# Three weight tiles of the first stage in buffers of another pool

## The chip, the cores and the metric

The kernel runs on one NeuronCore of a Trainium2 chip. A time is the device time of one execution in microseconds (us). The kernel before was timed three times: 1133.57, 1134.46 and 1135.39 us, median 1134.46. TensorE is called PE (its weight loads PEld), VectorE DVE, ScalarE ACT, GpSimd POOL. SyncE (SP) computes nothing here: it issues most of the DMAs, in the order of its own instruction stream, and what it waits for holds up every DMA behind it.

## The reference, cut to what matters

One layer of a backbone over 640 tokens (512 of a noisy grid, 128 of a prompt), width 1024, all in float32. What matters is the beginning:

```python
m = silu(cvec) @ w_ada + b_ada                  # modulation: 1024 -> 6 * 1024, for two vectors c and c_ctx
sh1, sc1, g1, sh2, sc2, g2 = split(m, 6)
h = rmsnorm(x, norm1_g) * (1.0 + sc1) + sh1
u_rw, u_na, gate_rw, gate_na = split(h @ p["w_in"], IN_SPLITS)
q, k, v = split(u_na, 3)                        # then the recurrence over u_rw, neighbourhood attention over q, k, v,
                                                # the merge, and a feed-forward block
```

The first stage needs only `sh1` and `sc1`, 2048 columns of `w_ada`: 8 MB of weights for two vectors. `h` is the input of every projection that follows.

## The kernel before, in words

Products of large matrices are done in three passes of a split float32: a weight tile of 512 KB is loaded into `wst` (`wdma`, L176), rounded by ACT into `whi` (L194), and what is left goes into `wlo` on DVE (L197); `h` is split likewise, into `hh` (ACT, L434) and `hl` (DVE, L436 and L438). There are two `wst` buffers.

**The first stage** (`with s0`). The modulation of `sh1` and `sc1` is cut by columns into three parts, `ada_part(k0, n, c0)`: part one covers the feature blocks 0 and 1 of the eight, part two blocks 2 and 3, part three blocks 4 to 7. Each part runs over all eight blocks of the inner dimension. Parts one and two load four tiles `wa` each (a tile holds two blocks of the inner dimension and comes in two DMAs of 256 KB), part three loads eight (one DMA of 512 KB each, `kt` 0 to 7). All have the tag `wa` of the stage's pool, with eight buffers (`WAB`): parts one and two take the eight, and tiles 0 to 3 of part three go where the tiles of part one were, tiles 4 to 7 where those of part two were. Each tile is used by one group of matmuls of PE into `psa` (`ada_mm`, L263). When a part is complete, `mod_part` copies its rows (L418), transposes them (L421), makes the coefficients A and B (L424, L427) and writes that part of `hh` and `hl`.

Between these groups PE does the first projection, q: `qg` is a generator of its matmuls (L313), four weight chunks of two inner blocks each, 60 matmuls for the first two chunks. `PRM["qp"]` says how many of them stand between two groups. In part two these are 0, 0, 7, 6 and 7, in part three 2, 5, 4, 4, 3, 2, 5, 3 and 1: the group of tile 0 follows the 2, that of tile 1 the 5, and so on, and the weights of the second q chunk are asked for between tiles 2 and 3. The third chunk needs blocks 4 and 5 of `h`, so it comes after part three.

**What sets the order.** In this stage PE's order is written by hand (`tc.manual_schedule(engines={PE})`). The order of SP, ACT, DVE and POOL is written by the framework's planner, ahead of the run: it goes through the program with times of its own, and gives an engine the instruction that comes first in the program among those that it holds to be ready. A DMA whose buffer is free can so stand far ahead of its place in the program. After the first stage comes the rest of q, k and v (planner's order on PE too), then attention, recurrence and feed-forward, where orders written by hand prevail; SP's is the planner's throughout.

**The recurrence's pool** `nf` is opened before the first stage. It has two buffers `f5` and one `nk5`, each of 128 x 1280 float32. Their first users before the change: `upw`, 256 KB of small weights (`prep_dma`, L617, in `nk5`; read by `prep_cast` in the eighth step of attention), and half of each of the first two weight tiles of the modulation's later columns (`ada_w`, L1027, in `f5`, 512 KB each; read by PE at L1046 from the first steps of attention on). The table `rpbp` comes in windows `win` of 124.5 KB (L860).

Of the kernel before, what the change touches and what calls it, by code (L numbers as in the profile page):

```python
# [7 lines left out]
F32 = mybir.dt.float32  # L8
# [6 lines left out]
P = 128  # L15
# [7 lines left out]
XB, WAB, FA, SF = 4, 8, 2, 16  # L23
# [87 lines left out]
def V(ap, dims, off=0):  # L111

    return bass.AP(ap.tensor, ap.offset + off, [list(ap.ap[0])] + [list(d) for d in dims])
# [3 lines left out]
def body(ctx: ExitStack, tc: tile.TileContext, xs, xp, cols, consts, w_ada, b_row, w_rw, w_qkv,  # L117
# [5 lines left out]
    def open_pool(stack, name, bufs=1, space=None):  # L123
        if space is None:
            return stack.enter_context(tc.tile_pool(name=name, bufs=bufs, reuse_waits="tile"))
        return stack.enter_context(tc.tile_pool(name=name, bufs=bufs, reuse_waits="tile", space=space))

    def right_pool(stack, name):
        return stack.enter_context(tc.tile_pool(name=name, bufs=1, reuse_waits="tile", side="right"))
# [14 lines left out]
    def nm(s):  # L144
        cn[0] += 1
        return f"{s}_{cn[0]}"
# [189 lines left out]
        dve.tensor_scalar(out=D[:, dqg:dqg + 1], in0=col("qg"), scalar1=0.125, scalar2=None,  # L336
                          op0=ALU.mult)


    hs = ExitStack()  # L340
    weights(ctx, WST, 2)
    o, mt = [], []
# [22 lines left out]
    nf = open_pool(nstack, "nf")  # L365
    nk_t = lambda n, shape: nf.tile(shape, F32, tag="nk5", bufs=1, name=nm(n))
    f5 = lambda: nf.tile([P, 1280], F32, tag="f5", bufs=2, name=nm("f5"))
    sb = open_pool(s1, "p1")
    p1 = sb
    kcT = sb.tile([P, 4, 128], F32, name="kcT")  # L370
# [5 lines left out]
    sb = right_pool(s0, "p0")  # L376
# [11 lines left out]

    def wa_load(k0, n, kt):

        w = sb.tile([P, 1024], F32, tag="wa", bufs=WAB, name=nm("wa"))
        for i in range(4 // n):
            wv = w_ada[(kt + i) * 128:(kt + i + 1) * 128, 0:2048].rearrange("p (g c) -> p g c", g=2)
            sp.dma_start(V(w[:, :], [[128 * n, 2], [1, 128 * n]], i * 256 * n), wv[:, :, 128 * k0:128 * (k0 + n)])
        return w

    def ada_part(k0, n, c0):

        for kt in range(0, 8, 4 // n):
            w = wa_load(k0, n, kt)  # L400
            yield
            for i in range(4 // n):
                ada_mm(psa, w[:, i * 256 * n:(i + 1) * 256 * n], kt + i, 64 * n, c0)
# [438 lines left out]
    with s1:  # L842

        s1.enter_context(s1l)
        sb = right_pool(s1l, "p1l")
# [90 lines left out]
        with ExitStack() as s1b:  # L936
# [128 lines left out]
            with tc.manual_schedule(engines=FIRST):  # L1065
                for k, step in enumerate(PRM["na"].split()):
                    a, p, b, q, n, s_ = (int(x) for x in (step + ".0").split(".")[:6])
# [31 lines left out]
    with ExitStack() as s3:  # L1099
        sb = open_pool(s3, "p3")  # L1100
# [653 lines left out]
    def add_gated(ps, i, n, c, a=0, b=512):  # L1754
# [15 lines left out]
                      name=f"b{x[0]}{x[1]}{i}") for i in range(2)] for x in halves2}  # L1770
    sb = open_pool(ctx, "p4")
# [466 lines left out]
    with tc.manual_schedule(engines=FIRST):  # L2238
# [8 lines left out]
        for part, fs in enumerate(fts):  # L2247
# [3 lines left out]
            for j, ft in enumerate(todo):  # L2251
# [13 lines left out]
                n = len(todo)  # L2265
# [114 lines left out]
def _build(arrays):  # L2380
    import concourse.bacc as _bacc

    nc = _bacc.Bacc("TRN2", target_bir_lowering=False, num_devices=1)
    args = [nc.dram_tensor(f"in_{n}_dram", v.shape, mybir.dt.from_np(v.dtype), kind="ExternalInput").ap()
            for n, v in arrays.items()]
    args += [nc.dram_tensor(f"out_{i}_dram", s, F32, kind="ExternalOutput").ap()
             for i, s in enumerate(_OUTS)]
    with tile.TileContext(nc, **TCARGS) as tc:
        body(tc, *args)
    return nc  # L2390
# [12 lines left out]
```

## Time and profile before

| | before |
|---|---|
| time, median of 3 runs | 1134.46 us |
| the profiled execution's own time | 1134.67 us |
| its span, first to last instruction | 1132.8 us |
| PE busy | 1099.7 us, 97% |
| DVE, ACT, POOL busy | 72%, 50%, 22% |
| mean granted clock of PE | 0.995 |
| bytes moved, mean rate | 179.05 MB, 158 GB/s |
| DMA in the stretch from 10 to 41 us | 16 engines busy throughout, 375 GB/s |

Busy time is the union of an engine's instructions; PE's ends are modelled, so its busy time is an upper bound of its work. A timeline gives the start in us from the first instruction, the duration, engine and line, the operation with what it writes and reads, how many are merged in the row, and in brackets how long the engine stood idle before and what ended that. "SPq" is the issue of a DMA, not its transfer.

### The profile page before, as it was taken

To read this page: it belongs to the slowest core of one execution; us is meant where nothing else is said; L and a number is where in the kernel's file an instruction comes from. 1 tells how busy PE (TensorE), PEld (TensorE's weight loads), DVE (VectorE), ACT (ScalarE), POOL (GpSimd) and SP (SyncE) were. 2 spreads that over 40 slices of the span, in tenths; PEclk is the share of its full clock that TensorE was granted. 3 is DMA by queue.
4 is the path that set the end of the run, shared out by engine and by line. 5 is a ranking of instruction groups with operands and counts; after the bars stand their busy time and mean duration, and the time that the engine had idled before them with its cause. 6 is when DMAs were issued, how large, how long until landed. Compare 5 with 4: busy or idle time off the path is not lost. (4 is left out here: it accounts for less than half of the span.)

```text
span 1132.8 us, 27124 instructions
## 1 busy us (share of the span) xinstructions
PE 1099.7 (97%) x11118; PEld 970.9 (86%) x11118; DVE 814.6 (72%) x1709; ACT 571.7 (50%) x1106; POOL 246.3 (22%) x318
## 2 busy tenths in 40 slices
PE   6999999999999999999999999999999999999998
PEld 4688878889888988888898788998999989989987
DVE  4565465668648947956697846899788888889854
ACT  4445566665566575467543524554453543444430
POOL 1163235321101111210100431152212122131200
PEclk8999999999999999999999999999999999999999
DMA  9753677645423353353643873377567567665622
GB/s 341 264 108 104 186 258 266 211 138 127 118 57 96 105 141 91 96 134 81 248 139 108 260 222 130 131 178 191 135 181 181 143 158 174 181 165 139 158 84 93
DMA packets 72995, 179.05 MB, mean 158 GB/s; under 512 B 8708, under 2 KB 23684, under 8 KB 72872
## 3 DMA queue, kind: packets, MB, share of 16 engines
q1 hardware_dynamic: 58488, 140.86, 37.8%
q0 software_dynamic: 12368, 33.56, 16.2%
q10 hardware_dynamic: 2016, 2.90, 0.8%
q8 instruction: 87, 1.43, 0.5%
q14 instruction: 36, 0.29, 0.1%
HBM read 137.81 MB, written 16.94 MB: 137 GB/s over the span
## 5 line engine op out<-in xcount | busy, mean ns | idle before, releaser
L1932 PE MATMUL f<-t,whi 128*128 128x320 f32 x640 | 141.8, 309 | 1.1 <-ACT whi L1977 0.8
L1932 PE MATMUL f<-b,whi 128*128 128x320 f32 x608 | 135.0, 310 | 0.4 <-DVE b L214 0.4
L225 PE MATMUL fl<-h,whi 128*128 128x320 f32 x672 | 122.5, 321 | 0.7 <-ACT U L542 0.7
L1932 PEld LDWEIGHTS f<-t,whi 128*128 128x128 f32 x640 | 106.8, 188 | 1.9 <-ACT whi L1977 1.3
L225 PEld LDWEIGHTS fl<-h,whi 128*128 128x128 f32 x672 | 101.2, 188 | 6.0 <-ACT U L542 0.9
L1932 PEld LDWEIGHTS f<-b,whi 128*128 128x128 f32 x608 | 101.8, 188 | 1.2 <-issue 0.6
L1932 PE MATMUL f<-t,wlo 128*128 128x320 f32 x320 | 99.0, 309 | 0.2 <-DVE wlo L1980 0.2
L1932 PE MATMUL f<-b,wlo 128*128 128x320 f32 x304 | 94.0, 309 | 0.1
L194 ACT CAST whi<-wst 128x1024 fp32r<-128x1024 f32 (+1 forms) x67 | 68.9, 1030 | 39.1 <-PE acc L313 27.1
L313 PE MATMUL acc<-whi,h 128*128 128x512 f32 x240 | 79.3, 404 | 0.3 <-DVE h L438 0.3
L1977 ACT CAST whi<-ws 128x1024 fp32r<-128x1024 f32 x40 | 42.1, 1052 | 68.7 <-PE f L1932 42.2
L197 DVE TENSOR_TENSOR wlo<-wst,whi 128x1024 fp32r<-128x1024 f32 (+2 forms) x47 | 48.1, 1033 | 26.0 <-ACT whi L194 25.8
L193 POOL DMA_DIRECT2D wlo<-wst x28 | 24.9, 889 | 183.7 <-ACT wlo L192 168.0
L225 PE MATMUL fl<-h,wlo 128*128 128x320 f32 x336 | 62.3, 317 | 0.0
L1932 PEld LDWEIGHTS f<-t,wlo 128*128 128x128 f32 x320 | 60.1, 188 | 0.5 <-DVE wlo L1980 0.5
L1991 POOL TENSOR_TENSOR ws<-wst 128x512 f32<-128x512 f32 x20 | 31.8, 1589 | 120.9 <-DVE wlo L1980 81.6
L1932 PEld LDWEIGHTS f<-b,wlo 128*128 128x128 f32 x304 | 57.1, 188 | 0.4 <-DVE wlo L1980 0.4
L1980 DVE TENSOR_TENSOR wlo<-ws,whi 128x1024 fp32r<-128x1024 f32 x40 | 53.7, 1343 | 4.1 <-ACT whi L1977 4.1
L313 PEld LDWEIGHTS acc<-whi,h 128*128 128x128 f32 x240 | 45.3, 191 | 12.7 <-issue 2.4
L1475 DVE TENSOR_TENSOR ZV<-w,Dt 64x128 f32<-64x128 f32 x64 | 18.5, 289 | 52.0 <-PE w L1463 50.9
L225 PEld LDWEIGHTS fl<-h,wlo 128*128 128x128 f32 x336 | 51.2, 188 | 1.8
L984 POOL TENSOR_TENSOR L<-L,m 128x384 f32<-128x384 f32 (+1 forms) x40 | 32.1, 824 | 93.8 <-DVE m L983 75.8
(379 smaller groups left out, 2826.4 us busy)
## 6 DMA issues: line engine op xcount, KB each, us to landing
wst<-in_w_dram SPq DMA_DIRECT2D x58, 512.0 KB
wst<-in_w_rw_dram SPq DMA_DIRECT2D x31, 512.0 KB
wlo<-wst POOLq DMA_DIRECT2D x28, 512.0 KB, 4.6
wa<-in_w_ada_dram SPq DMA_DIRECT2D x24, 512.0 KB
f<-in_w_ada_dram SPq DMA_DIRECT2D x16, 512.0 KB
t<-in_w_dram SPq DMA_DIRECT2D x16, 512.0 KB
wst<-in_w_qkv_dram SPq DMA_DIRECT2D x12, 512.0 KB
o<-o_d SPq DMA_DIRECT2D x14, 320.0 KB
```

The lines of the kernel that those rows point to most:

```text
L193: pool.dma_start(lo[:, :n].bitcast(F32), st[:, :n], accum_op=ALU.add)
L194: act.copy(hi[:, :n], st[:, :n])
L197: dve.tensor_tensor(out=lo[:, a:b], in0=st[:, a:b], in1=hi[:, a:b].bitcast(F32), op=ALU.subtract)
L225: pe.matmul(ps[:, :t1 - t0], w[:, a:a + 128], x[:, k0 + kt, t0:t1], start=n == 0, stop=n == 3 * nk - 1)
L313: pe.matmul(pss[i][:, a:b], lhs(x, kt, ts_), w[:, cs_], start=ki == 0 and n == 0, stop=ki == last and n == 2)
L984: pool.tensor_tensor(out=L, in0=L, in1=V(m[:, :], [[0, w]], 3), op=ALU.mult)
L1475: dve.tensor_tensor(out=V(ZV[own, l + 1, h, :], [[128 * dl, 2], [1, 64]]), in0=V(pn[own, :], [[64, 2], [1, 64]], 64 * g), in1=V(Dt[own, 0, ...
L1932: pe.matmul(ps[:, :H2], w_[:, c_], x_[:, kt, :], start=first and kt + n == 0, stop=last and kt == 3 and n == 2, skip_group_check=more)
L1977: act.copy(r[0][:, :width], src())
L1980: dve.tensor_tensor(out=r[1][:, :width], in0=src(), in1=r[0][:, :width].bitcast(F32), op=ALU.subtract)
L1991: eng_x(PRM["se"][i - 1]).tensor_tensor(out=o_, in0=x, in1=y, op=op)
```

## The change

The loader of the modulation's tiles, `wa_load`, takes the buffers of tiles 4, 5 and 6 of part three (`n == 4` is part three) from the pool `nf`: tiles 4 and 5 are the first users of the two buffers `f5`, tile 6 is the first of `nk5`. Of each the first 1024 columns are used. The other five tiles of part three stay in the stage's pool, where tile 7 now is the fifth and not the eighth that asks for a buffer again. `upw` and the two `f` tiles become the second users of their buffers, and wait for the groups of matmuls that read tiles 6, 4 and 5. Sizes of pools, transfers and the work of all engines are the same.

```diff
     nk_t = lambda n, shape: nf.tile(shape, F32, tag="nk5", bufs=1, name=nm(n))
     f5 = lambda: nf.tile([P, 1280], F32, tag="f5", bufs=2, name=nm("f5"))
+    late_home = (f5, f5, lambda: nk_t("wa", [P, 1280]))
...
     def wa_load(k0, n, kt):
 
-        w = sb.tile([P, 1024], F32, tag="wa", bufs=WAB, name=nm("wa"))
+        w = late_home[kt - 4]()[:, 0:1024] if n == 4 and 3 < kt < 7 else sb.tile([P, 1024], F32, tag="wa", bufs=WAB, name=nm("wa"))
         for i in range(4 // n):
             wv = w_ada[(kt + i) * 128:(kt + i + 1) * 128, 0:2048].rearrange("p (g c) -> p g c", g=2)
             sp.dma_start(V(w[:, :], [[128 * n, 2], [1, 128 * n]], i * 256 * n), wv[:, :, 128 * k0:128 * (k0 + n)])
```

## Rows read from the trace of the kernel before

**Rows 1.** The page's first part: busy time, share of span, instructions of each engine.

```profile
PE 1099.7 (97%) x11118; PEld 970.9 (86%) x11118; DVE 814.6 (72%) x1709; ACT 571.7 (50%) x1106; POOL 246.3 (22%) x318
```

**Rows 2.** Stretches: busy us per engine, PE's clock, DMA share, GB/s; sum from 45 us.

```profile
35.00:40.00 5.00, 4.00 (x33) 1.63 (x31) 2.13 (x6) 1.05 (x1) 0.00 (x0) 1.00 1.04 393
40.00:45.00 5.00, 4.95 (x39) 2.24 (x35) 0.56 (x1) 0.00 (x0) 0.61 (x2) 1.00 0.73 279
...
45.00:145.00 100.00, 99.88 (x552) 82.67 (x553) 55.73 (x118) 51.78 (x103) 37.43 (x41) 1.00 0.51 137
...
sum 1087.00, PE 1066.34 PEld 951.35 DVE 794.81 ACT 553.95 POOL 242.09; mean PE 133.29 PEld 118.92 DVE 99.35 ACT 69.24 POOL 30.26
```

**Rows 3.** Timeline of PE from 18 to 45 us.

```profile
18.96 2.63 PE L263 MATMUL psa<-wa,cs 128*32 128x128 f32 x32
...
35.90 0.50 PE L313 MATMUL acc<-whi,h 128*128 128x512 f32 x1
...
37.02 0.64 PE L263 MATMUL psa<-wa,cs 128*32 128x256 f32 x8
...
39.55 0.64 PE L263 MATMUL psa<-wa,cs 128*32 128x256 f32 x8 [0.99 <-DMA wa<-in_w_ada_dram]
...
40.90 0.64 PE L263 MATMUL psa<-wa,cs 128*32 128x256 f32 x8
...
42.83 0.64 PE L263 MATMUL psa<-wa,cs 128*32 128x256 f32 x8
...
44.31 0.64 PE L263 MATMUL psa<-wa,cs 128*32 128x256 f32 x8
```

**Rows 4.** Timeline of SP's DMA issues from 20 to 34 us.

```profile
20.91 0.34 SPq L176 DMA_DIRECT2D wst<-in_w_qkv_dram  x1
21.66 2.52 SPq L860 DMA_DIRECT2D win<-in_rpbp_dram  x2
24.41 0.40 SPq L394 DMA_DIRECT2D wa<-in_w_ada_dram  x1
25.10 0.35 SPq L617 DMA_DIRECT2D upw<-in_lup_dram  x1
26.46 1.68 SPq L1027 DMA_DIRECT2D f<-in_w_ada_dram  x2
29.85 0.33 SPq L176 DMA_DIRECT2D wst<-in_w_qkv_dram  x1
31.16 2.51 SPq L394 DMA_DIRECT2D wa<-in_w_ada_dram  x4
```

**Rows 5.** SP's waits, 20 to 46 us.

```profile
SPq L394 <- DMA wst<-in_w_qkv_dram: 0.9, 1, 0.9
```

**Rows 6.** Two more stretches, columns as in rows 2.

```profile
31.16:39.55 8.39, 7.39 (x53) 3.49 (x51) 4.91 (x15) 4.25 (x6) 0.00 (x0) 1.00 1.04 399
...
41.00:46.00 5.00, 4.88 (x36) 2.38 (x37) 0.46 (x2) 0.00 (x0) 0.00 (x0) 1.00 0.53 200
```

**Rows 7.** DMAs issued from 10 to 41 us: count, KB each.

```profile
f<-in_w_ada_dram SPq DMA_DIRECT2D x2, 512.0 KB
...
upw<-in_lup_dram SPq DMA_DIRECT2D x1, 256.0 KB
win<-in_rpbp_dram SPq DMA_DIRECT2D x2, 124.5 KB
```

**Rows 8.** Timeline of ACT and DVE from 31 to 39 us.

```profile
31.12 1.05 ACT L194 CAST whi<-wst 128x1024 fp32r<-128x1024 f32 x1 [3.09 <-DMA wst<-in_w_qkv_dram]
...
32.20 1.22 DVE L197 TENSOR_TENSOR wlo<-wst,whi 128x1024 fp32r<-128x1024 f32 x1 [0.44 <-ACT whi L194]
...
34.26 1.29 DVE L438 TENSOR_TENSOR h<-ht,h 128x512 fp32r<-128x512 f32 x2
...
38.25 1.05 ACT L194 CAST whi<-wst 128x1024 fp32r<-128x1024 f32 x1 [3.89 <-DMA wst<-in_w_qkv_dram]
```

**Rows 9.** Timeline of PE at the first use of a tile f.

```profile
139.87 0.62 PE L1046 MATMUL psa<-f,cs 128*32 128x512 f32 x2
```

## The prediction

> **What bounds the kernel now.** The page comes first: PE is busy for 1099.7 us of 1132.8 [rows 1], so a change elsewhere is worth what PE idles for it. The second view is the busy time by stretches around the change. From 45 to 145 us PE has 0.12 us of idle time; from 35 to 40 us it has 1.00, from 40 to 45 us 0.05 [rows 2]. The third view, PE's timeline, says what the 1.00 is: one wait of 0.99 us for a DMA into `wa`, before the group of matmuls at 39.55 us. It is the fifth group of part three, tile 4; tiles 3 to 7 start at 37.02, 39.55, 40.90, 42.83 and 44.31 [rows 3]. The granted clock is 1.00 there, the 2.4 GHz level [rows 2], so it plays no part.
>
> Why is tile 4 late? SP's timeline answers, and not with the buffer. Tile 4 goes where part two's first tile was, and the matmuls on part two's first two tiles ended at 18.96 + 2.63 = 21.59 us [rows 3], but its DMA was issued at 31.16 [rows 4]. What SP waited for just then is the landing of the q weights issued at 20.91 [rows 5], and ACT's cast of those starts at 31.12, the moment they are there [rows 8]. So the DMA engines are the limit: 10 us from issue to use, with the engines fully busy at 399 GB/s in the 8.4 us behind it [rows 6]. A tile lands when all that was queued before it has landed. Before tile 4 stand, from 20.91 on: the q weights, two windows, tile 3, `upw`, two tiles `f`, the next q weights [rows 4]. `upw` and the `f` tiles are the odd ones: the first `f` is read at 139.87 us [rows 9], `upw` in a later step than that. They are early only because the planner held their buffers to be free and tile 4's not.
>
> **The change, part by part.** *The three loads in other buffers.* Tiles 4, 5 and 6 have no earlier user now. In the planner's eyes they are ready at once, and first in the program among the ready ones, so I expect them right behind the q weights of 20.91, about where the windows stand now. `upw` and both `f` tiles cannot be issued before the groups of tiles 6, 4 and 5 have run on PE. So 256 + 2 x 512 KB = 1.31 MB [rows 7] leave the queue ahead of these groups, which is 1.31 MB / 399 GB/s = 3.3 us [rows 6].
>
> When does tile 4 land? One tile of 512 KB takes 0.524 MB / 399 GB/s = 1.31 us. At the latest it keeps its place behind all else: 39.5 - 3.3 = 36.2 us. At the earliest it follows the q weights: 31.1 + 1.3 = 32.4 us. PE comes to its group 1.48 us after tile 3's, as from tile 6's to tile 7's, where also three projection matmuls lie between (42.83 to 44.31) [rows 3]: at 37.02 + 1.48 = 38.50 us. Both ends lie before, so the wait goes whichever place the planner takes. Tile 7 by the same count lands, at the latest, four tiles behind the cast at 38.25 [rows 8] and 3.3 us sooner: 38.25 + 5.2 - 3.3 = 40.2 us, and is wanted at about 43.2.
>
> *What it gives.* From tile 3's to tile 4's group 2.53 us become 1.48: 1.06 us. From tile 4's to tile 5's it is 1.35 us with two matmuls between. A matmul takes (1.93 - 1.48) / 2 = 0.23 us (40.90 to 42.83 has five between, 42.83 to 44.31 three), so 1.25 would do: 0.10 us, the rest of a short wait for tile 5. From there the rhythm is already PE's own. Sum: 1.15 us.
>
> *What stands behind it.* The chain after tile 7 is PE's rows, their copy, transposes, `h`: it starts 1.15 us sooner and waits for nothing of the DMA. The q weights cast at 38.25 [rows 8] may land later than now, since tiles 5 to 7 can pass them: at most three tiles less the 3.3 us, 0.6 us, and they are wanted only after part three, beyond 45 us. After 45 us PE has no idle time for 100 us [rows 2], so what is gained is neither lost to another engine nor enlarged there. Bounds of the term: nothing below 0 from the wait itself; at most all of PE's idle time from 35 to 45 us, 1.05 us, and some 0.1 of weight loads. I take 1.15.
>
> *The loads that are moved back.* `f`, `f` and `upw` become possible when the groups of tiles 4, 5 and 6 are done, at about 39.1, 40.4 and 42.3 us. From 41 to 46 us the DMA engines are busy for 0.53 of the time [rows 6], so 2.3 us are free, and from 45 us on half. The 3.3 us of transfers fit before 50 us, and the first of them is wanted at 139.87 us [rows 9]. Cost: nothing; that cover of 90 us doesn't go.
>
> *SP's queue.* The three now wait for PE, and what SP holds behind them waits too. By the trace such a wait costs nothing here: the next q and k weights are limited by `wst` buffers, and PE has no wait from 45 to 145 us [rows 2]. The Trainium skill, "Perfetto Trace Analysis", section "DMA Instruction — HWDGE (DVE, Sync)", says that on trn2 the DMA engines don't wait for semaphores: the wait sits in the issuing sequencer, ahead of the descriptors. It speaks against the change, for `upw` would hold whatever stands behind it until 42.3 us; by it the sum would change only if tile 7 stood behind `upw`, issued at 42.4, landed no sooner than 43.7 and 0.5 us late, a gain of 0.6 and 1133.9 us. By the rows tile 7 stands earlier in the program and its buffer is free from 21.59 us, so I leave the sum at 1.15.
>
> **Rivals.** *The wait moves to tile 3 (or another early tile).* Tile 3 needs part one's last buffer, and the planner put it behind the two windows [rows 4]: it held that buffer to be taken until then. Now three tiles are ready in that gap. If all three and the windows go first, tile 3 lands at 31.1 + 3 x 1.31 + 0.6 (windows, 0.25 MB) + 1.31 = 37.0 us, just when PE wants it (37.02). With up to 0.8 us of scatter this leaves a gain of 0.4 to 1.2: 1133.3 to 1134.1 us. Against it: two full tiles give the planner as much time as two windows did.
>
> *Slower: the second q weights fall behind the new tiles.* Place: SP's queue at 20.91 us. If tiles 4 to 6 go before the `wst` load, it lands 3.9 us later, and the cast at 31.12 with it. On DVE `wlo`, then both steps of `h` stand in one line behind the cast [rows 8], so the first `hl` (now 34.26 + 0.65 = 34.9) comes at 38.8. PE wants it for the matmul of 35.90, the second of that chunk, which begins 0.9 us before [rows 3]: 2.9 us lost, 1.15 gained, +1.8 us. With tile 3 too in front it is four tiles, 5.2 us: +3.1. So 1136.3 to 1137.6, middle 1136.9. It decides from three tiles on: one late tile (1.3 us) costs 0.3 us. For it: these tiles wait for nothing. Against: the load comes earlier in the program, and its buffer is free too.
>
> *The planner draws another order later on.* It plans with its own times, and these have shifted; SP's order is its own to the end, and after the first stage for a while PE's too. For it: PE is busy for 1066.34 of the 1087 us from 45 us on [rows 2], so 20.7 us of idle time lie there. Against: PE has none in the stretch where its own order is the planner's. I price it at 3.5 us either way, an estimate: about a sixth of these, 1129.8 or 1136.8.
>
> *It doesn't do what it says.* If SP's order stayed as it is, with `upw` and `f` ahead, they would wait for matmuls on tiles that stand behind them; that order can't be run. So the loads do move. Chance close to nothing.
>
> **How the numbers follow.** The profiled execution took 1134.67 us, 1.87 more than its span, and 0.21 above the median. 1134.67 - 1.15 = 1133.52; from the median, 1134.46 - 1.15 = 1133.3 us, which I forecast. Chances: the forecast 0.60 (its own range 1132.7 to 1133.9); the wait moved to tile 3 or given back later 0.16; q weights late 0.11; another order later 0.12, half on each side; no effect 0.01. About 0.2%, 2.3 us, is what a measurement of this kernel can tell from no change: faster is below 1132.2, slower above 1136.7. Faster: the better half of the redrawn orders and a tail of the forecast, 0.12. Slower: two thirds of the late q weights and half of the redrawn orders, with some of what I don't see, 0.15. Same 0.73. The range from 1131.5 to 1136.7 leaves about 1 in 10 on each side.
>
> **What would show it.** Right: SP's timeline has three more loads of `wa` behind 20.91 and before 29, and `upw` and `f` behind about 39 us; the wait of 0.99 at tile 4 is gone, and the groups of tiles 3 to 7 stand 1.48, 1.25, 1.93 and 1.48 us apart; the stretch from 45 us on looks as before, some 1.2 us sooner. Wrong: ACT's second cast later than 32 us with a wait of PE near 35 (q weights late), a wait of PE at the fourth group (tile 3 late), or PE's matmuls at 45 us earlier by 1.2 but the end not, which would mean that a later stage isn't bound by PE.

## The result and the profile after

The changed kernel takes 1138.35 us in the median of 13 runs (1134.77 to 1141.10), the kernel before 1133.9 beside it (1131.73 to 1136.29): a ratio of 1.0037 with a 95% interval of 1.0023 to 1.0050, slower by 2.6 to 5.7 us. The forecast was 1133.3, with a range up to 1136.7: it was wrong.

The profiled execution of the changed kernel took 1138.35 us, its span is 1136.2. The first part of its page, as [rows 1], shows PE no busier in sum than before:

```profile
PE 1100.7 (97%) x11118; PEld 973.2 (86%) x11118; DVE 811.7 (71%) x1709; ACT 571.5 (50%) x1106; POOL 244.4 (22%) x318
```

**The first stage did what was forecast.** SP's issues after the change, from 21 to 42 us (compare [rows 4]; tiles 4 and 5 are called `f` now, since they lie in those buffers; the two `wa` at 23.45 are tiles 3 and 6; tile 7 was issued at 29.97):

```profile
21.04 0.34 SPq L176 DMA_DIRECT2D wst<-in_w_qkv_dram  x1
21.80 1.56 SPq L394 DMA_DIRECT2D f<-in_w_ada_dram  x2
23.45 1.59 SPq L394 DMA_DIRECT2D wa<-in_w_ada_dram  x2
26.03 1.91 SPq L860 DMA_DIRECT2D win<-in_rpbp_dram  x2
28.74 0.35 SPq L176 DMA_DIRECT2D wst<-in_w_qkv_dram  x1
...
38.42 1.56 SPq L1027 DMA_DIRECT2D f<-in_w_ada_dram  x2
41.58 0.33 SPq L617 DMA_DIRECT2D upw<-in_lup_dram  x1
```

PE's groups of tiles 3 to 7 after the change (timeline; compare [rows 3]), and the stretches of [rows 2]:

```profile
36.26 0.64 PE L263 MATMUL psa<-wa,cs 128*32 128x256 f32 x8
...
37.72 0.64 PE L263 MATMUL psa<-f,cs 128*32 128x256 f32 x8
...
38.95 0.64 PE L263 MATMUL psa<-f,cs 128*32 128x256 f32 x8
...
40.88 0.64 PE L263 MATMUL psa<-wa,cs 128*32 128x256 f32 x8
...
42.36 0.64 PE L263 MATMUL psa<-wa,cs 128*32 128x256 f32 x8
```

```profile
35.00:40.00 5.00, 5.00 (x39) 2.36 (x36) 1.02 (x3) 1.05 (x1) 0.00 (x0) 1.00 0.86 288
40.00:45.00 5.00, 4.88 (x33) 2.64 (x32) 1.84 (x9) 0.45 (x1) 0.61 (x2) 1.00 0.93 341
45.00:145.00 100.00, 100.00 (x563) 83.12 (x563) 55.65 (x116) 53.20 (x105) 37.11 (x42) 1.00 0.52 143
```

The wait at tile 4 is gone and the groups stand 1.46, 1.23, 1.93 and 1.48 us apart. Matmul by matmul, PE is 1.95 us ahead of the trace before from tile 5 on. Of this 0.76 us stood already at tile 3 (37.02 against 36.26), since the granted clock was lower in the trace before from 19 to 26 us (0.51 against 1.00); the rest, 1.19, is the change's. Up to 660 us the lead is between 1.7 and 3.5 us, and there it is 2.08.

**The loss lies at 669 us**, in the output projection. PE multiplies there by `w_out`, in chunks of 512 KB numbered 0 to 7. For chunks 0 to 4 the low part isn't subtracted on DVE: ACT writes the negative of the rounded weights (L192), and an accumulating DMA issued by POOL adds the weights to it (L193). PE's timeline where it comes to the low part of chunk 3, after the change:

```profile
668.25 0.65 PE L1781 MATMUL pc<-K,arow 2*128 2x2 f32 x8
672.68 0.50 PE L313 MATMUL acc<-wlo,m 128*128 128x512 f32 x1 [3.77 <-DMA wlo<-wst]
...
673.48 0.55 PE L313 MATMUL acc<-wlo,m 128*128 128x512 f32 x1
...
674.68 0.63 PE L313 MATMUL acc<-wlo,m 128*128 128x512 f32 x1
```

and the stretches of the wait and behind it (seventh number: PE's granted clock):

```profile
668.90:672.68 3.78, 0.01 (x1) 0.00 (x1) 0.00 (x0) 0.00 (x0) 0.00 (x0) 1.00 0.92 246
672.68:676.40 3.72, 3.72 (x11) 2.92 (x12) 1.38 (x2) 0.00 (x0) 0.00 (x0) 0.62 0.69 225
```

Before, the same matmul begins with no wait:

```profile
670.92 0.50 PE L313 MATMUL acc<-wlo,m 128*128 128x512 f32 x1
```

Behind the 3.77 us the granted clock is 0.62 in the mean, partly the 1.2 GHz level; until PE is at 2.4 GHz again it loses another 1.6 us. PE's lead of 2.08 becomes a lag of 3.37: 5.4 us lost, and nothing later moves it.

**Where the low part was held up.** SP's issues around it, before (first fence) and after (second):

```profile
632.79 1.85 SPq L1711 DMA_DIRECT2D tr<-trw_d  x4
634.68 11.08 SPq L176 DMA_DIRECT2D wst<-in_w_out_dram  x3
...
655.37 0.33 SPq L176 DMA_DIRECT2D wst<-in_w_out_dram  x1
...
657.57 1.78 SPq L1746 DMA_DIRECT2D x<-in_xs_dram  x4
```

```profile
630.50 0.32 SPq L1564 DMA_DIRECT2D mx<-trw_d  x1
640.57 0.33 SPq L176 DMA_DIRECT2D wst<-in_w_out_dram  x1
640.96 2.89 SPq L1711 DMA_DIRECT2D tr<-trw_d  x4
643.91 0.92 SPq L176 DMA_DIRECT2D wst<-in_w_out_dram  x2
...
657.37 0.33 SPq L176 DMA_DIRECT2D wst<-in_w_out_dram  x1
...
658.53 1.78 SPq L1746 DMA_DIRECT2D x<-in_xs_dram  x4
```

The planner drew SP's order anew here, some 600 us behind the change. Taken instruction by instruction, it is the only place behind the first stage where SP's order differs, and one load has moved. Before, four `tr` loads (320 KB each) go first, then chunks 1, 2 and 6 (the row of 634.68: chunks 1 and 2 at once, chunk 6 at 645.43, when its buffer is free). After, chunk 6, which is needed after all of these, stands first; it waits until 640.57 for its buffer, and the four `tr` loads and chunks 1 and 2 wait behind it. ACT then waits for chunk 1, for which it had no wait before:

```profile
650.20 1.06 ACT L192 ACTIVATE wlo<-wst 128x1024 fp32r<-128x1024 f32 x1 [2.92 <-DMA wst<-in_w_out_dram]
```

Chunk 3's load comes for the same reason at 657.37, right behind the landing of chunk 1's accumulating DMA (657.30; 655.01 before). The accumulating DMAs (L193, from 640 to 690 us) now need up to 9.2 us from issue to landing; before it was 7.2 in the same window (first fence before, second after):

```profile
DMA to landing us min/median/max: 5.3/5.9/7.2
```

```profile
DMA to landing us min/median/max: 5.7/6.0/9.2
```

### The profile page after: what moved, and what is told of

It reads as the page before. It is cut to its first block, busy times and chain, and to the rows that moved or that the text cites. A ratio compares the mean times of both kernels' runs of the same rounds, so it can differ in the third digit from the quotient of the medians.

```text
span 1136.2 us, 27125 instructions
## 1 busy us (share of the span) xinstructions
PE 1100.7 (97%) x11118; PEld 973.2 (86%) x11118; DVE 811.7 (71%) x1709; ACT 571.5 (50%) x1106; POOL 244.4 (22%) x318
## 5 line engine op out<-in xcount | busy, mean ns | idle before, releaser
L193 POOL DMA_DIRECT2D wlo<-wst x28 | 24.9, 890 | 186.8 <-ACT wlo L192 171.1
```

Of the source, the lines that this page charges most:

```text
L193: pool.dma_start(lo[:, :n].bitcast(F32), st[:, :n], accum_op=ALU.add)
```

## The experiments

The pin `pin(a, b)` in the diffs plans DMA `a` behind DMA `b` in SP's order; it adds no wait of its own. `wo[q]` is the load of `w_out`'s chunk q, `tr` the four `tr` loads. The theory going in: the first stage gives some 2 us, and the redrawn order at the output projection costs some 5.5. Each was timed in five rounds.

**The order put back.**

```diff
+# at the load of w_out's chunk 6, in wdma
+pin(wo[6], wo[2])
```

> The changed kernel, but SP's load of w_out's chunk 6 is held behind that of chunk 2, where the kernel before has it; the first stage is left as the change makes it. Theory (the redrawn order of SP's loads at the output projection costs some 5.5 us there, and the first stage gives some 2): PE's wait of 3.77 us before the group on w_out[3] and the slow matmuls behind it go, PE stays about 2 us ahead of the kernel before to the end, and the time is 1131.3 to 1132.5 us. Rival A (PE, 2 us earlier, only meets loads of the output projection that were limited by their transfers anyway): the wait stays at 2 us or more, and the time is 1134 to 1138. Rival B (the loss is the drop of the clock and not the order): the clock drops all the same, 1137 or more.

1131.62 us against 1134.06, ratio 0.9983 (0.9970 to 0.9996). PE at the same place, without a wait:

```profile
670.26 0.50 PE L313 MATMUL acc<-wlo,m 128*128 128x512 f32 x1
```

The whole loss is gone with the place of one load (with it the planner also put the casts of chunks 1 and 2 on ACT one cast of `m` sooner). By the time rivals A and B fall. In this execution PE is only 0.66 us ahead of the trace before and not the 2 expected, so the row alone would not tell against rival A; the next experiment does. Where PE doesn't wait, the clock stays up (1.00 from 668 to 676 us).

**The order alone**, in the kernel before.

```diff
+for t in tr: pin(t, wo[6])
+pin(wo[1], tr[3]); pin(wo[2], tr[3])
```

> The kernel before, first stage untouched, but with the changed kernel's later order of SP's loads: chunk 6 of w_out ahead of the four tr loads, chunks 1 and 2 behind them. Theory: the whole loss and none of the gain, a wait of 3 to 4 us on w_out[3]'s low part and 1 to 2 us of matmuls at the lower clock behind it: 1138 to 1140.5 us. Rival A (the loss comes from PE being 2 us earlier, and not from the order): 1133.5 to 1135, no wait there.

1140.38 us (6 runs) against 1134.06, ratio 1.0062 (1.0047 to 1.0078): the loss without the gain, 5.3 to 8.8 us. In the profiled execution PE loses 5.6 us at this place, the wait and the lowered clock behind it; what else it is longer than the trace before comes earlier. PE here isn't early, and waits as long:

```profile
678.49 0.50 PE L313 MATMUL acc<-wlo,m 128*128 128x512 f32 x1 [3.94 <-DMA wlo<-wst]
```

**The bytes moved, the buffers as before.** (In this kernel the planner also redrew the later order in the same way, so it carries the pin of the first experiment; two instructions of DVE are exchanged.)

```diff
+# first stage, the kernel before: its own eight buffers
+pin(upw, wa[7]); pin(f[0], wa[7]); pin(f[1], wa[7])
+pin(wo[6], wo[2])
```

> The kernel before with its own eight buffers in the first stage, but the loads of upw and of the first two f are held behind tile 7's, and chunk 6 of w_out is held in the place that the kernel before gives it. Theory (what the first stage gives comes from the 1.31 MB that leave the queue ahead of tiles 4 to 7, and not from the three extra buffers): tile 4 lands by 36 to 38 us, its wait of 0.99 goes, PE at 54 us is 1 to 2.3 us earlier than before, 1131.8 to 1133.2 us. Rival C (the extra buffers themselves give it): no gain at 41 us, 1133.7 to 1134.5 us.

1131.70 us, ratio 0.9981 (0.9967 to 0.9995): the same gain as with the extra buffers. SP's issue of tiles 4 to 7, and PE's groups of tiles 3, 4 and 7 there:

```profile
26.49 5.06 SPq L394 DMA_DIRECT2D wa<-in_w_ada_dram  x4
```

```profile
38.73 0.64 PE L263 MATMUL psa<-wa,cs 128*32 128x256 f32 x8
...
40.19 0.64 PE L263 MATMUL psa<-wa,cs 128*32 128x256 f32 x8
...
44.83 0.64 PE L263 MATMUL psa<-wa,cs 128*32 128x256 f32 x8
```

The four tiles are issued from 26.49 us on and not from 31.16 [rows 4]. By the semaphore of its DMA tile 4 lands at 37.00 us, as expected, against 39.50 in the kernel before. PE's rows alone don't show that: it is 6.10 us from tile 3 to tile 7, as in the changed kernel (42.36 - 36.26) and against 7.29 before, but PE itself came later in this execution (the granted clock was 0.73 from 19 to 26 us), to tile 4 at 40.19, when that tile was there in the kernel before too. For the same reason "PE at 54 us is 1 to 2.3 us earlier" missed; it is 0.5 later there. The landing and the time together say that the 1.31 MB are enough; rival C falls.

**The low part of chunk 3 on DVE**, with the redrawn order left in place.

```diff
-            ws.append(src if isinstance(src, (tuple, list)) else wload(src, eng))
+            ws.append(src if isinstance(src, (tuple, list)) else wload(src, None if ci == 3 else eng))
```

> The changed kernel with its redrawn order, but the low part of w_out[3] is subtracted on DVE and not by ACT with an accumulating DMA. Theory (the late order hurts through that one DMA, which shares the engines with the x and G loads): the wait of 3.77 us goes but for a few tenths, as its cast on ACT ends near 663 us, the clock stays up, 1132 to 1133.5 us. Rival D (everything behind the blocked load is late, and PE waits for the x or G loads or for the weight's own load in its place): 1136 to 1138.5 us.

1131.57 us, ratio 0.9979 (0.9967 to 0.9991). DVE subtracts at 659.73 and PE doesn't wait:

```profile
659.73 1.22 DVE L197 TENSOR_TENSOR wlo<-wst,whi 128x1024 fp32r<-128x1024 f32 x1 [6.46 <-PE acc L313]
```

So the late order costs time through one accumulating DMA. Two controls: the same edit in the kernel before,

> Control: the kernel before, with w_out[3]'s low part subtracted on DVE. Theory (DVE's subtraction helps only where the accumulating DMA is late, and in the kernel before it is not): 1133.3 to 1134.8 us, no gain. Rival (the DVE form is faster by itself, so that the run of the changed kernel with it said nothing about the order): 1131 to 1132.5 us.

gave 1132.38 against 1133.29, ratio 0.9993 (0.9980 to 1.0005): no gain that this measurement tells, though it can't exclude a small one. With both cures in the changed kernel,

> Both cures in the changed kernel: chunk 6 of w_out held behind chunk 2, and w_out[3]'s low part on DVE. Theory (each cure alone takes the whole loss away, so that the second adds nothing): 1131.2 to 1132.4 us, as either alone. Rival (each leaves a part of the loss): 1129 to 1130.8 us.

1131.97, ratio 0.9986 (0.9973 to 0.9998): not better than either alone.

**Half the order put back**: the `tr` loads first again, chunks 1 and 2 still behind chunk 6.

```diff
+pin(wo[6], tr[3])
+pin(wo[1], wo[6]); pin(wo[2], wo[6])
```

> The changed kernel, with only half of its later order put right: the four tr loads go back ahead of the load of w_out's chunk 6, while w_out's chunks 1 and 2 stay behind it. Theory (the loss runs through the weights: chunks 1 and 2 behind the blocked load, so their casts, so the buffer and the load of chunk 3, so its accumulating DMA): the wait on w_out[3]'s low part stays at 2.5 to 4 us, 1136.5 to 1139.5 us. Rival (it runs through the tr loads, whose late casts hold ACT): the wait goes, 1131.3 to 1133 us.

1131.07 against 1133.29, ratio 0.9987 (0.9974 to 1.0000): the theory missed, and its rival had the time but for 0.2 us. SP, PE and the landing of the L193 DMAs in that run (three views):

```profile
628.74 1.86 SPq L1711 DMA_DIRECT2D tr<-trw_d  x4
638.42 2.19 SPq L176 DMA_DIRECT2D wst<-in_w_out_dram  x3
...
651.29 0.33 SPq L176 DMA_DIRECT2D wst<-in_w_out_dram  x1
```

```profile
667.15 0.50 PE L313 MATMUL acc<-wlo,m 128*128 128x512 f32 x1 [0.25 <-DMA wlo<-wst]
```

```profile
DMA to landing us min/median/max: 4.8/5.3/6.7
```

Chunk 6 blocks SP here too, until 638.42, and little comes of it. Chunk 1, issued behind it at 638.81, lands at 644.69, and ACT comes to it at 645.03 without a wait:

```profile
645.03 1.06 ACT L192 ACTIVATE wlo<-wst 128x1024 fp32r<-128x1024 f32 x1
```

PE is 2.0 us earlier in this trace than in the changed kernel's (group of 20 matmuls at 652.10 against 654.11). Beside that, chunk 3's load is issued 657.37 - 651.29 - 2.0 = 4.1 us earlier. So the blocked load alone isn't the cause; it is the `tr` loads caught behind it, with 1.31 MB and 2.89 us of SP's time ahead of chunks 1 and 2. They were not late for their own users: in the changed kernel DVE goes over from `pre` to `tr` at 646.70 with no wait. So the rival had the time but not the path.

**The `tr` loads last**, to test that reading.

```diff
+pin(wo[1], wo[6]); pin(wo[2], wo[1])
+for t in tr: pin(t, wo[2])
```

> The changed kernel, with the load of w_out's chunk 6 first, as the change makes it, then w_out's chunks 1 and 2, and the four tr loads behind these: the tr loads are still later than in the changed kernel, but their 1.31 MB no longer stand ahead of the two weight chunks. Theory now (the loss is the 1.31 MB and SP's 2.9 us ahead of chunks 1 and 2): the cast of chunk 1 no longer waits 2.9 us for its load, w_out[3]'s low part is not late by more than 0.5 us, 1131 to 1133.5 us unless PE waits for tr itself. Rival (late tr loads do the harm, by their casts on ACT or their adds on DVE): PE or ACT waits 3 us or more in this stretch, 1136 us or more.

1136.12 us against 1132.88, ratio 1.0033 (1.0019 to 1.0048). The theory missed, and the waits and the time are those that the rival named: ACT waits 5.50 us, DVE 3.79 us for the first `tr`. But ACT's wait is not for `tr`. The planner, which holds chunk 1 to be early now, put its cast on ACT ahead of six casts of `m`, and ACT waits there for the load; PE then waits for `m`, and the clock falls again. PE itself has no wait for `tr`. ACT, DVE and PE in that run:

```profile
643.87 1.06 ACT L192 ACTIVATE wlo<-wst 128x1024 fp32r<-128x1024 f32 x1 [5.50 <-DMA wst<-in_w_out_dram]
```

```profile
647.53 0.49 DVE L1718 SCALAR_TENSOR_TENSOR tr<-tr,fl 128x320 f32<-128x320 f32 x1 [3.79 <-DMA tr<-trw_d]
```

```profile
645.33 0.49 PE L313 MATMUL acc<-whi,m 128*128 128x512 f32 x1 [2.28 <-ACT m L1721]
647.06 0.79 PE L313 MATMUL acc<-whi,m 128*128 128x512 f32 x1 [1.24 <-POOL m L1722]
...
671.89 0.50 PE L313 MATMUL acc<-wlo,m 128*128 128x512 f32 x1
```

The low part of chunk 3 is in time (671.89, no wait), as the theory had it. But over these waits PE loses 5.3 us against the trace before, so that it comes there later, and the row bears out nothing.

The order brought in a wait of its own, so it doesn't settle how the harm is shared between the bytes of `tr` and SP's time for issuing them. That stays open.

**A version that beats the changed kernel** is any of three: that kernel with the first pin, with the half order, or with DVE's subtraction. They stand 1.5 to 2.4 us under the kernel before (the interval of the half order reaches no change) and can't be told from each other.

## Why the prediction was wrong, point by point

- *The three loads in other buffers*: right. SP's order, the tiles' distances (1.46, 1.23, 1.93, 1.48 for 1.48, 1.25, 1.93, 1.48) and the vanished wait came out as worked. By the semaphores of their DMAs tile 4 landed at 31.15 us, ahead of the 32.4 that was its earliest, since the q weights ahead of it landed at 29.90 and not at 31.1. Tile 3, for which the first rival had 37.0 us, landed at 33.92, 2.3 us ahead of its use. That the gain is the 1.31 MB and not the buffers was its argument, and the third experiment bears it out.
- *What it gives, 1.15 us* (2.53 less 1.48 is 1.05 and not 1.06; the sum stays): 1.19 by the traces, from tile 3 to tile 7. In time the first stage gives 1.9 us (0.5 to 3.4, first experiment), which includes 1.15. Yet the step "The granted clock is 1.00 there [...] so it plays no part" looked only at 35 to 45 us. From 19 to 26 us the clock was 0.51 in the trace before, and it sets when PE comes to tile 4, not when the tile lands. In the kernel with the first stage as before and a clock of 1.00 there (the order alone), tile 4 starts at 39.70, as at 39.55 [rows 3], and PE waits longer for it; with the change and a clock of 1.00 it starts with PE, at 37.72. From tile 3 to tile 7 the two take 10.36 and 6.10 us: at that clock the change gives 4.3 us and not 1.19. So 1.15 was the price of one draw, a trace with a low clock. Stretch 19 to 26 us and tile 4, the order alone:

```profile
19.00:26.00 7.00, 5.46 (x65) 3.42 (x63) 5.30 (x15) 3.33 (x6) 0.84 (x1) 1.00 1.08 367
```

```profile
39.70 0.64 PE L263 MATMUL psa<-wa,cs 128*32 128x256 f32 x8 [2.68 <-DMA wa<-in_w_ada_dram]
```

- *The loads that are moved back* and *SP's queue*, within the first stage: right, PE has no idle time from 45 to 145 us.
- *What stands behind it* is the step that failed: "what is gained is neither lost to another engine nor enlarged there" rested on the 100 us behind the stage. The loss is 630 us later. It is the rival *The planner draws another order later on*, on its slower side, which had a chance of 0.06. Its price was 3.5 us, a sixth of PE's idle time: a share of idle time that is already there doesn't price a wait that isn't there yet. It cost 3.77 us of wait and 1.6 of lowered clock in the trace; alone it costs 5.3 to 8.8 us (second experiment).
- The argument against that rival, "PE has none in the stretch where its own order is the planner's", was about PE's order. The one that was redrawn to harm is SP's, and SP's is the planner's to the end, as the prediction itself said.
- The prediction cited the Trainium skill, "Perfetto Trace Analysis", section "DMA Instruction — HWDGE (DVE, Sync)", for a wait that sits in the issuing sequencer, and took from it that such a wait holds what stands behind it. It set this aside for the first stage, rightly. At 640.57 us this trace agrees with it: the `tr` loads are issued from 0.39 us behind the load that waited, and not from 632.79 as before.

The shift of the planner was not read out of the profile, and could not be: the trace before holds one order. What it could have told is how little room there is here: SP waited 9.6 us in one piece for an accumulating DMA at this place before the change too, and in the kernel before the low part of chunk 3 landed at 670.69, 0.2 us ahead of its use.

## What to carry to other kernels

Where a planner writes a queue's order, a small edit can change that order far from the edit, and that can cost more than the edit gives; compare the whole order of each queue before and after, and pin the few loads whose places matter. A load that must wait for a buffer belongs behind those that needn't and are wanted sooner. And a gain read from one execution is one draw: where PE races a DMA, ask how it comes out at either clock.

## What the runs showed of the hardware

**An accumulating DMA started later, the more SP's queue still had to move.** Counted from the DMA records, for chunk 3's low part: from POOL's issue to its first packet, the bytes that SP's queue moved in that time, and from the first packet to the last.

```
kernel                 to first packet   SP's queue moved   first to last
tr loads last               1.46 us           320 KB            2.74 us
order put back              1.94 us           796 KB            3.91 us
before                      2.45 us          1008 KB            3.41 us
half order                  2.64 us          1084 KB            3.70 us
order alone                 4.24 us          1656 KB            4.31 us
after                       4.64 us          1500 KB            4.23 us
```

The middle column counts over the delay itself, so it grows with it. What SP's queue had been given and not yet moved when POOL issued is free of that: 324, 1040, 1056, 1244, 2132 and 2204 KB in the order of the table. With nothing moving on SP's queue an accumulating DMA of the changed kernel (636.05 us) took 1.48 us to its first packet.

That is the last link of the loss. Against the half order, and with PE's 2.0 us taken off, the DMA is issued 1.0 us later, starts another 2.0 later and takes 0.5 longer: 3.5 us, which is 3.77 less 0.25. The Trainium skill, "DMA: Bandwidth & Descriptors", section "Queues, rings and completion order", says that each DMA engine takes turns between its queues, packet by packet. Once both were moving they did share (596 KB of SP's queue in the 4.23 us); before that none of its packets moved for up to 4.64 us. Whether it got no turn or wasn't ready, the runs don't show.

**The longer waits of PE cost about one and a half times themselves.** Behind the 3.77 us the matmuls ran at the 1.2 GHz level for a while and lost another 1.6 us; behind the 3.94 us of the order alone it was 1.6 too, and 1.6 behind its 2.68 us at tile 4 (10.36 us less 6.10 and 2.68), behind the two waits of 2.28 and 1.24 us in the last experiment 1.8. Behind the 0.25 us of the half order and the 0.99 us of tile 4 in the trace before the clock stayed at 1.00.
